# The decode tokens' small steps in both mixers, per head or tile before, for four heads or four tiles together after

## The chip, the cores and the metric

One core of a Trainium2 chip runs the kernel. Its engines are TensorE (PE), VectorE (DVE), ScalarE (ACT), GpSimd (POOL) and the sync engine (SP), which here issues every DMA. The metric is the device time of one execution in microseconds: 1788.39 us before, the median of three runs (1786.42 to 1792.95).

## What is computed

One step of a two-layer network in float32: a prompt of 512 tokens and eight decode tokens, one each of eight sequences with states of their own. Layer 0 has a gated delta rule (GDN) as mixer, layer 1 a state-space scan (SSD); each is followed by a layer norm, a convolutional feed-forward part and another norm. What a decode token needs of the two mixers is one step of their recurrences:

```python
# GDN: per head, state s (DK x DV); q, k l2-normalised, q also scaled by DK ** -0.5
s = exp(g) * s
v_new = beta * (v - k @ s)
o = q @ s + (q . k) * v_new
s = s + outer(k, v_new)

# SSD: per head, state h (P x N); B, C shared by the heads of a group
h = exp(dt * a) * h + dt * outer(x, B)
y = h @ C + D * x
```

The l2 norm of a row t is `t * rsqrt(sum(t * t) + 1e-6)`. In SSD the kernel uses that `y = exp(dt*a) * (h @ C) + dt * x * (B . C) + D * x`, with the old h.

## The kernel before

All 520 tokens go as columns through the weight matmuls, in two halves of 260 (`HT`). A unit is one 128-row tile of outputs: 24 matmuls per half (three for each of eight 128-row tiles of inputs, since weights and inputs are split into a high and a low fp32r part). `prep` loads a weight tile, ScalarE makes `hi` (L223), and VectorE or GpSimd makes `lo` (L224); three tiles are held at a time. The units run in the order of `plan`; between them stand the mixers' own steps.

In GDN the loop over eight heads runs three units (q, k and v columns of the head), copies the decode columns into `kqv`, calls `gdn_decode` for them, and then `gdn_head` and four `gdn_chunk` for the prompt. `gdn_head` multiplies `Xe` on GpSimd (L769), sums it on VectorE to `Ac` (L771), writes that to DRAM, reads it back as `D` and inverts the diagonal blocks by a chain of steps `Xtmp` (L812); after that come triangular solves with small matmuls into `XT`, and the chunks with `st`, `w`, `o`. `gdn_norm` transposes the head's result (`ot`).

`gdn_decode` for one head: GpSimd forms k k and k q (`pr`, 128x8 each) and q q (`qd2`); a matmul with ones sums them over the partitions into PSUM, VectorE copies them to `dk` (L941). k and q are transposed and sent through DRAM (`kr`), to be read back broadcast over the partitions (`kb`, four DMAs of 256 KB a head). GpSimd multiplies these by the old states (L952), VectorE sums each product over its last axis into `ks` (L953). Then eight 128x8 steps on VectorE (L959, L961 to L965, L967 to L969) and one power on GpSimd (L536, exponent -0.5 from the tile `halves`) give `vn` and `ud`. The states themselves are updated later, within the feed-forward part, from `vn`. After the last head `gdn_decode_norm` norms `ud` for heads 0 to 3 and then 4 to 7, and the output projection starts.

In SSD a group g of the four has B, C and four tiles of x, each of two heads. `ssd_group` runs after the group's sixth unit: chunk states, then `ssd_bcast` (B and C of the decode tokens transposed, their product summed on VectorE on eight partitions, L1210 and L1211, and sent through DRAM to `bcd` on all partitions), and then per tile the prompt's decays `sE`, scores `yd` and `yo`, and `ssd_decode`: state times C (GpSimd or VectorE, L1237), summed into `dy` (L1238), three 128x8 steps (L1240 to L1242), and a fourth (L1243) that adds the result into the decode columns of x. The z units that read x come after the next group's six units, in the last group after four others.

The tile framework's scheduler orders the instructions of each engine before the run, by the order of the code, priorities and a timeline of its own, and sets the semaphores. Each engine then works through its list in order.

## Time and profile before

| what | value |
|---|---|
| median of 3 runs | 1788.39 us |
| profiled execution | 1785.41 us |
| its span, first to last instruction | 1783.6 us |
| TensorE busy | 1613.7 us (90%), 12889 matmuls |
| VectorE busy | 1221.2 us (68%), 2133 instructions |
| ScalarE busy | 839.3 us (47%), 1724 |
| GpSimd busy | 968.4 us (54%), 1090 |
| chain that ended last, by engine | PE 30%, DVE 24%, DMA 18%, POOL 14%, ACT 8%, issue 5% |

In forty slices of the span (44.6 us each; a digit is the busy share in tenths) TensorE and VectorE read `8888899888999899999888897989988998889997` and `5967888668876544337699989895569765554356`. GDN lies in the slices 2 to 9, SSD in 20 to 28; the long plateaus of TensorE between and behind them are the feed-forward parts. Matmuls are pipelined, so a busy TensorE is not one at its peak; idle time of an engine that nobody waits for costs nothing.

### The profile page before, as it was taken

The numbers are of one execution on the slowest core, as the hardware profiler recorded it, in microseconds if no ns is written. First come the engines' busy times: TensorE is split into PE (matmuls) and PEld (weight loads), VectorE is DVE, ScalarE is ACT, GpSimd is POOL, SyncE is SP. The second block draws the span as 40 slices with busy tenths as digits, with TensorE's granted clock in tenths as the row PEclk, the third lists the DMA queues.
The fourth block names the chain that finished last, engine by engine and source line by source line (L and its number), as shares of the span: only waits on it lengthen the run. The fifth ranks groups of instructions, "written<-read, shape, count | busy, mean of one in ns | idle before, by whom it ended". The sixth has DMA issues, their size and how long they took to land.

```text
span 1783.6 us, 33737 instructions
## 1 busy us (share of the span) xinstructions
PE 1613.7 (90%) x12889; PEld 1550.4 (87%) x12889; DVE 1221.2 (68%) x2133; ACT 839.3 (47%) x1724; POOL 968.4 (54%) x1090
## 2 busy tenths in 40 slices
PE   8888899888999899999888897989988998889997
...
DVE  5967888668876544337699989895569765554356
...
DMA packets 108978, 250.36 MB, mean 140 GB/s; under 512 B 15344, under 2 KB 31696, under 8 KB 108784
## 3 DMA queue, kind: packets, MB, share of 16 engines
...
## 4 chain that ended last, share of the span: by engine, by line
PE 30%; DVE 24%; DMA 18%; POOL 14%; ACT 8%; issue 5%; SPq 1%; ACTq 0%; DVEq 0%; POOLq 0%
PE psl L246 26%; DVE lo L224 3%; DMA raw<-w_up 3%; DMA Sr<-bd 3%; POOL Sd L990 3%; ACT hi L223 3%; POOL Sr L988 3%; DVE sE L1180 2%; DMA Sr<-kr 2%; DVE y L419 2%; DMA raw<-w_down 2%; POOL Sd L989 2%; POOL fl L279 1%; DVE Xtmp L812 1%; DMA Sd<-sstate 1%
## 5 line engine op out<-in xcount | busy, mean ns | idle before, releaser
L246 PE MATMUL psl<-XH,hi 128*128 128x260 f32 (+1 forms) x2816 | 819.5, 292 | 61.4 <-ACT u L442 18.4
L246 PE MATMUL psl<-XL,hi 128*128 128x260 f32 (+1 forms) x2848 | 823.6, 290 | 8.8 <-DVE lR L308 3.9
L246 PE MATMUL psl<-XH,lo 128*128 128x260 f32 (+1 forms) x2816 | 809.7, 288 | 2.7 <-DVE lo L224 1.6
L246 PEld LDWEIGHTS psl<-XH,hi 128*128 128x128 f32 (+1 forms) x2816 | 538.9, 192 | 78.0 <-ACT u L442 22.0
L224 DVE TENSOR_TENSOR lo<-raw,hi 128x512 fp32r<-128x512 f32 (+2 forms) x439 | 356.9, 850 | 327.7 <-ACT hi L223 323.3
L246 PEld LDWEIGHTS psl<-XL,hi 128*128 128x128 f32 (+1 forms) x2848 | 545.6, 192 | 15.4 <-issue 5.7
L246 PEld LDWEIGHTS psl<-XH,lo 128*128 128x128 f32 (+1 forms) x2816 | 539.2, 192 | 7.6 <-DVE lo L224 3.1
L223 ACT CAST hi<-raw 128x512 fp32r<-128x512 f32 (+2 forms) x499 | 315.2, 671 | 435.0 <-PE psl L246 191.7
L246 PE MATMUL psl<-fh,lo 128*128 128x260 f32 x704 | 201.2, 286 | 1.8 <-DVE lo L224 1.4
L246 PE MATMUL psl<-fh,hi 128*128 128x260 f32 x704 | 200.3, 284 | 0.7 <-ACT hi L223 0.7
L246 PE MATMUL psl<-fl,hi 128*128 128x260 f32 x704 | 198.8, 282 | 0.0
L224 POOL TENSOR_TENSOR lo<-raw,hi 128x1024 fp32r<-128x1024 f32 x60 | 148.6, 2476 | 53.5 <-ACT hi L223 52.1
L246 PEld LDWEIGHTS psl<-fh,lo 128*128 128x128 f32 x704 | 132.5, 188 | 4.0 <-DVE lo L224 3.6
L246 PEld LDWEIGHTS psl<-fh,hi 128*128 128x128 f32 x704 | 132.5, 188 | 1.4 <-ACT hi L223 0.9
L246 PEld LDWEIGHTS psl<-fl,hi 128*128 128x128 f32 x704 | 132.4, 188 | 0.2
L279 POOL TENSOR_TENSOR fl<-f,fh 128x260 fp32r<-128x260 f32 x88 | 80.3, 914 | 66.4 <-ACT fh L278 66.3
L419 DVE SCALAR_TENSOR_TENSOR s<-u,par,s 128x512 f32<-128x512 f32 x88 | 82.6, 939 | 6.8 <-ACT s L416 6.8
L278 ACT CAST fh<-f 128x260 fp32r<-128x260 f32 x88 | 36.0, 409 | 96.5 <-DVE f L481 96.5
L246 PE MATMUL psl<-y,hi 128*128 128x260 f32 x256 | 73.3, 288 | 1.8 <-DVE y L279 0.8
L990 POOL TENSOR_TENSOR Sd<-Sd,Sr 128x512 f32<-128x512 f32 x48 | 70.1, 1460 | 0.5
L365 POOL TENSOR_TENSOR lnsq<-lnsq,sq 128x260 f32<-128x260 f32 x48 | 46.8, 978 | 28.8 <-ACT sq L363 27.3
L471 POOL COPY cout<-u 128x10 f32<-128x10 f32 x44 | 19.2, 436 | 77.7 <-ACT u L442 77.6
...
## 6 DMA issues: line engine op xcount, KB each, us to landing
...
```

The lines of the kernel that those rows point to most:

```text
L223: nc.scalar.copy(out=hi[:, ks, :mw], in_=raw[:, ks, :])
L224: eng.tensor_tensor(out=lo[:, ks, :mw], in0=raw[:, ks, :], in1=hi[:, ks, :mw].bitcast(F32), op=ALU.subtract)
L246: self.nc.tensor.matmul(out=ps[h][:mw], lhsT=w[:, b0 + k, :mw], rhs=x[:, hs], start=(k0 + k == first and i == 0), stop=(k0 + k == last and ...
L278: nc.scalar.copy(out=hi, in_=xf)
L279: (eng or nc.gpsimd).tensor_tensor(out=lo, in0=xf, in1=hi.bitcast(F32), op=ALU.subtract)
L365: nc.gpsimd.tensor_tensor(out=acc, in0=acc, in1=sq, op=ALU.add)
L419: nc.vector.scalar_tensor_tensor(out=y[:, :S], in0=u[:, j:j + S], scalar=self.pcol(wname, i * w + j), in1=y[:, :S], op0=ALU.mult, op1=ALU.add)
L471: nc.gpsimd.tensor_copy(out=cout[:, m, :], in_=u[:, 2 + S - 2:2 + T])
L988: nc.gpsimd.tensor_tensor(out=t, in0=t, in1=_bc(col[:, :, None], D4), op=ALU.mult)
L989: nc.gpsimd.tensor_tensor(out=St, in0=St, in1=_bc(decay[:, :, None], D4), op=ALU.mult)
L990: nc.gpsimd.tensor_tensor(out=St, in0=St, in1=t, op=ALU.add)
L1180: nc.vector.tensor_scalar(out=E[:, c, :], in0=E[:, c, :], scalar1=self.acum[:, c, h:h + 1], scalar2=0.0, op0=ALU.subtract, op1=ALU.min)
```

## The change

GDN: `gdn_decode` keeps what starts the DMAs (transpose, `kr`, `kb`, multiplies and sums, now into the tile `kS` of all heads). The products, the ones matmul, the power and the eight steps move into `gdn_decode_rest`, which is called twice, after `gdn_head` of head 4 for heads 0 to 3 and after that of head 7 for heads 4 to 7, on 128x32 operands. The sums are copied from PSUM by ScalarE instead of VectorE. SSD: `dy` holds the four tiles of a group, and three 128x32 steps and the four final ones run in `ssd_decode_rest` at the group's end. The product B C is formed by GpSimd on all partitions and summed by a matmul with ones; two DMAs a group go. `halves` shrinks to one column per exponent, broadcast by the access pattern. The line numbers behind the change are up to 16 higher.

```diff
...
         nc.sync.dma_start(out=self.par, in_=a["par"])
-        self.halves = p.tile([P, 2, B], F32, name="halves")
-        nc.vector.memset(self.halves[:, 0], -0.5)
-        nc.vector.memset(self.halves[:, 1], 0.5)
+        self.halves = p.tile([P, 2], F32, name="halves")
+        nc.vector.memset(self.halves[:, :1], -0.5)
+        nc.vector.memset(self.halves[:, 1:], 0.5)
         self.mean = p.tile([P, P], F32, name="mean")
...
         n = x.shape[-1]
-        self.nc.gpsimd.tensor_tensor(out=y, in0=x, in1=self.halves[:, which, :n], op=ALU.pow)
+        self.nc.gpsimd.tensor_tensor(out=y, in0=x, in1=_bc(self.halves[:, which:which + 1], [P, n]), op=ALU.pow)
 
...
                     x = self.gdn_head(p, h, st["kq", h], st["v", h], e)
+                    if h in (NA, H - 1):
+                        self.gdn_decode_rest(p, *((0, NA) if h == NA else (NA, H)))
                     for c in range(C):
...
         self.kqv = p.tile([P, H, 3, B], F32, name="kqv")
+        self.kS = p.tile([P, H, 2, B], F32, name="kS")
         self.vn = self.keep.tile([P, H, B], F32, tag="k0", name="vn")
...
         kqv = self.kqv[:, h]
-        k, q, vd = (kqv[:, t, :] for t in range(3))
-        pr = p.tile([P, 2, B], F32, tag="pr", name="pr", bufs=2)
-        nc.gpsimd.tensor_tensor(out=pr[:, 0, :], in0=k, in1=k, op=ALU.mult)
-        nc.gpsimd.tensor_tensor(out=pr[:, 1, :], in0=k, in1=q, op=ALU.mult)
-        nc.gpsimd.tensor_tensor(out=self.qd2[:, h, :], in0=q, in1=q, op=ALU.mult)
         ps = self.sp("dks")
-        nc.tensor.matmul(out=ps[:, P:P + 2 * B].rearrange("p (t b) -> p t b", t=2), lhsT=self.ones, rhs=pr, start=True, stop=True)
         self.transpose(ps[:2 * B, :P], kqv[:, :2, :].rearrange("p t b -> p (t b)"))
...
         nc.scalar.copy(out=rows, in_=ps[:2 * B, :P])
-        dk = p.tile([P, 2, B], F32, tag="dk", name="dk", bufs=2)
-        nc.vector.tensor_copy(out=dk, in_=ps[:, P:P + 2 * B].rearrange("p (t b) -> p t b", t=2))
         kr = self.dram.tile([2, B, P], F32, tag=f"kr{h}", name="kr")
         nc.sync.dma_start(out=kr.rearrange("t b d -> (t b) d"), in_=rows)
-        ks = p.tile([P, 2, B], F32, tag="ks", name="ks", bufs=2)
+        ks = self.kS[:, h]
         for i in range(2):
...
                 nc.vector.tensor_reduce(out=ks[:, t, bs], in_=m, axis=AX.X, op=ALU.add)
-        ps2 = dk
-        sm = p.tile([P, 4, B], F32, tag="sm", name="sm", bufs=2)
-        rk, t, _, t2 = (sm[:, i, :] for i in range(4))
-        vn = self.vn[:, h, :]
-        egh, bh = self.deg[:, h, :], self.dbeta[:, h, :]
-        nc.vector.tensor_scalar(out=t, in0=ps2[:, 0, :], scalar1=1e-6, scalar2=None, op0=ALU.add)
-        self.power(t, rk, 0)
-        nc.vector.tensor_tensor(out=t, in0=rk, in1=egh, op=ALU.mult)
-        nc.vector.tensor_tensor(out=t, in0=t, in1=ks[:, 0, :], op=ALU.mult)
-        nc.vector.tensor_tensor(out=vn, in0=vd, in1=t, op=ALU.subtract)
-        nc.vector.tensor_tensor(out=vn, in0=vn, in1=bh, op=ALU.mult)
-        nc.vector.tensor_tensor(out=vn, in0=vn, in1=rk, op=ALU.mult)
-        u = self.ud[:, h, :]
-        nc.vector.tensor_tensor(out=t, in0=ks[:, 1, :], in1=egh, op=ALU.mult)
-        nc.vector.tensor_tensor(out=t2, in0=vn, in1=ps2[:, 1, :], op=ALU.mult)
-        nc.vector.tensor_tensor(out=u, in0=t, in1=t2, op=ALU.add)
         for i in range(2):
...
 
+    def gdn_decode_rest(self, p, h0, h1):
+
+        nc = self.nc
+        n = h1 - h0
+        hs = slice(h0, h1)
+        k, q, vd = (self.kqv[:, hs, t, :] for t in range(3))
+        ks = self.kS[:, hs]
+        pr = p.tile([P, 2, n, B], F32, tag="pr", name="pr", bufs=1)
+        nc.gpsimd.tensor_tensor(out=pr[:, 0], in0=k, in1=k, op=ALU.mult)
+        nc.gpsimd.tensor_tensor(out=pr[:, 1], in0=k, in1=q, op=ALU.mult)
+        nc.gpsimd.tensor_tensor(out=self.qd2[:, hs, :], in0=q, in1=q, op=ALU.mult)
+        ps = self.sp("drms")[:, :2 * n * B]
+        nc.tensor.matmul(out=ps, lhsT=self.ones, rhs=pr.rearrange("p t h b -> p (t h b)"), start=True, stop=True)
+        dk = p.tile([P, 2, n, B], F32, tag="dk", name="dk", bufs=1)
+        nc.scalar.copy(out=dk, in_=ps.rearrange("p (t h b) -> p t h b", t=2, b=B))
+        sm = p.tile([P, 3, n, B], F32, tag="sm", name="sm", bufs=1)
+        rk, t, t2 = (sm[:, i] for i in range(3))
+        vn, u = self.vn[:, hs, :], self.ud[:, hs, :]
+        eg, bh = self.deg[:, hs, :], self.dbeta[:, hs, :]
+        tt = lambda o, x, y, op: nc.vector.tensor_tensor(out=o, in0=x, in1=y, op=op)
+        nc.vector.tensor_scalar(out=t, in0=dk[:, 0], scalar1=1e-6, scalar2=None, op0=ALU.add)
+        flat = lambda x: x.rearrange("p h b -> p (h b)")
+        self.power(flat(t), flat(rk), 0)
+        tt(t, ks[:, :, 0, :], eg, ALU.mult)
+        tt(t, t, rk, ALU.mult)
+        tt(vn, vd, t, ALU.subtract)
+        tt(vn, vn, bh, ALU.mult)
+        tt(vn, vn, rk, ALU.mult)
+        tt(t, ks[:, :, 1, :], eg, ALU.mult)
+        tt(t2, vn, dk[:, 1], ALU.mult)
+        tt(u, t, t2, ALU.add)
+
     def gdn_state(self, p, after, h, i, kr):
...
         bcs = self.ssd_bcast(p, g, Bt, Ct)
+        yd4 = p.tile([P, 4, B], F32, tag="dy", name="dy", bufs=2)
         for q in range(4):
...
                 nc.sync.dma_start(out=ea[64 * s:64 * s + 64], in_=self.ade[h0 + s].rearrange("c t -> (c t)").partition_broadcast(64))
-            self.ssd_decode(p, g, q, x, bcs)
+            self.ssd_decode(p, g, q, x, bcs, yd4)
             d = self.pcol("sd", 4 * g + q)
...
             nc.gpsimd.tensor_tensor(out=x[:, P:S], in0=x[:, P:S], in1=ea[:, P:], op=ALU.add)
+        self.ssd_decode_rest(p, g, bcs[1], yd4)
 
...
         nc.scalar.copy(out=bc, in_=ps[:B, :2 * P].rearrange("p (t n) -> p t n", t=2))
-        t = p.tile([B, P + 1], F32, tag="bct", name="bct", bufs=2)
-        nc.vector.tensor_tensor(out=t[:, :P], in0=bc[:, 0, :], in1=bc[:, 1, :], op=ALU.mult)
-        nc.vector.tensor_reduce(out=t[:, P:], in_=t[:, :P], axis=AX.X, op=ALU.add)
+        t = p.tile([P, 2, B], F32, tag="bcd", name="bcd", bufs=2)
+        nc.gpsimd.tensor_tensor(out=t[:, 0], in0=Bt[:, S:], in1=Ct[:, S:], op=ALU.mult)
+        nc.tensor.matmul(out=ps[:, 2 * P:2 * P + B], lhsT=self.ones, rhs=t[:, 0], start=True, stop=True)
+        nc.scalar.copy(out=t[:, 1], in_=ps[:, 2 * P:2 * P + B])
         bd = self.dram.tile([2, B, P], F32, tag=f"bd{g}", name="bd")
...
             nc.sync.dma_start(out=bd[i], in_=bc[:, i, :])
-        cd = self.dram.tile([B, 1], F32, tag=f"cd{g}", name="cd")
-        nc.sync.dma_start(out=cd, in_=t[:, P:])
         c = p.tile([P, B, P], F32, tag="cbc", name="cbc", bufs=2)
         nc.sync.dma_start(out=c, in_=bd[1].rearrange("b n -> (b n)").partition_broadcast(P))
-        d = p.tile([P, B], F32, tag="bcd", name="bcd", bufs=2)
-        nc.sync.dma_start(out=d, in_=cd.rearrange("b o -> (b o)").partition_broadcast(P))
-        return c, d, bd
+        return c, t[:, 1], bd
 
-    def ssd_decode(self, p, g, q, x, bcs):
+    def ssd_decode(self, p, g, q, x, bcs, y):
 
...
         nc.vector.tensor_tensor(out=xd, in0=x[:, S:], in1=self.ddt[:, :, 0, i], op=ALU.mult)
-        y = p.tile([P, B], F32, tag="dy", name="dy", bufs=2)
-        t = p.tile([P, B], F32, tag="dyt", name="dyt", bufs=2)
         for j in range(2):
...
             (nc.vector if (i + j) % 3 == 2 else nc.gpsimd).tensor_tensor(out=Sd, in0=Sd, in1=c[:, bs], op=ALU.mult)
-            nc.vector.tensor_reduce(out=y[:, bs], in_=Sd, axis=AX.X, op=ALU.add)
+            nc.vector.tensor_reduce(out=y[:, q, bs], in_=Sd, axis=AX.X, op=ALU.add)
             self.later.append((self.ssd_state, i, j, bd))
-        nc.vector.tensor_tensor(out=y, in0=y, in1=self.ddt[:, :, 1, i], op=ALU.mult)
-        nc.vector.tensor_tensor(out=t, in0=xd, in1=cb, op=ALU.mult)
+
+    def ssd_decode_rest(self, p, g, cb, y):
+
+        nc = self.nc
+        gs = slice(4 * g, 4 * g + 4)
+        t = p.tile([P, 4, B], F32, tag="dyt", name="dyt", bufs=2)
+        nc.vector.tensor_tensor(out=y, in0=y, in1=self.ddt[:, :, 1, gs].rearrange("p b i -> p i b"), op=ALU.mult)
+        nc.vector.tensor_tensor(out=t, in0=self.xdd[:, gs], in1=_bc(cb[:, None, :], [P, 4, B]), op=ALU.mult)
         nc.vector.tensor_tensor(out=y, in0=y, in1=t, op=ALU.add)
-        nc.vector.scalar_tensor_tensor(out=x[:, S:], in0=x[:, S:], scalar=self.pcol("sd", i), in1=y, op0=ALU.mult, op1=ALU.add)
+        for q in range(4):
+            x = self.Y(4 * g + q)[:, S:]
+            nc.vector.scalar_tensor_tensor(out=x, in0=x, scalar=self.pcol("sd", 4 * g + q), in1=y[:, q], op0=ALU.mult, op1=ALU.add)
```

The scheduler places the instructions of both mixers anew; those of the two feed-forward parts stand as before. Three places, each before and then now.

VectorE, head 0 of GDN: from the decode chain to the reduction `Ac`, the start of the head's inversion.

```order
L963 TENSOR_TENSOR vn<-kqv,sm 128x8
L964 TENSOR_TENSOR vn<-vn,dbeta 128x8
L965 TENSOR_TENSOR vn<-vn,sm 128x8
L968 TENSOR_TENSOR sm<-vn,dk 128x8
L953 TENSOR_REDUCE ks<-kb 128x4
L967 TENSOR_TENSOR sm<-ks,deg 128x8
L914 TENSOR_SCALAR nt<-sq 128x4
L969 TENSOR_TENSOR ud<-sm 128x8
L771 TENSOR_REDUCE Ac<-Xe 128x64
```

```order
L768 TENSOR_TENSOR gbc<-gbc,kqk 128x256
L419 SCALAR_TENSOR_TENSOR kq<-u,par,kq 128x512
L948 TENSOR_REDUCE kS<-kb 128x4
L774 TENSOR_REDUCE Ac<-Xe 128x64
L775 TENSOR_TENSOR Ac<-Ac,Xi 128x64
```

The chain of head 0 has left the rows ahead of `Ac`; the sum into `kS` (L948, then L953) stays.

GpSimd, end of GDN: the powers (`halves`) and the last head's four multiplies into `kb`; L580 multiplies a head's result by z.

```order
L536 TENSOR_TENSOR nf<-nt,halves 128x4
L536 TENSOR_TENSOR sm<-sm,halves 128x8
L952 TENSOR_TENSOR kb<-kb,Sd 128x512 x3
L580 TENSOR_TENSOR R<-R,z 128x260
L580 TENSOR_TENSOR R<-R,z 128x252
L952 TENSOR_TENSOR kb<-kb,Sd 128x512
L582 COPY R<-z 128x8
```

```order
L536 TENSOR_TENSOR nf<-nt,halves 128x4
L921 TENSOR_TENSOR uo<-uo,nf 128x512
L947 TENSOR_TENSOR kb<-kb,Sd 128x512 x4
L580 TENSOR_TENSOR R<-R,z 128x260
L580 TENSOR_TENSOR R<-R,z 128x252
L582 COPY R<-z 128x8
L536 TENSOR_TENSOR nf<-nt,halves 128x4
L536 TENSOR_TENSOR sm<-sm,halves 128x32
L947 TENSOR_TENSOR kb<-kb,Sd 128x512 x4
```

One power of 32 columns now stands ahead of head 7's multiplies, where one of eight columns stood. On TensorE the last head's `ot` transposes stand behind 1,674 unit matmuls of the program, 1,620 before; the 96 of the output projection's first part end at 1,680 in both.

VectorE, group 1 of SSD: the steps of `dy` (`xdt`, `ea`, `sE` and `Sn` belong to the prompt).

```order
L1238 TENSOR_REDUCE dy<-Sd 128x4
L1154 TENSOR_TENSOR xdt<-xtk,dt 128x4x128
L1240 TENSOR_TENSOR dy<-dy,ddt 128x8
L1154 TENSOR_TENSOR xdt<-xtk,dt 128x4x128
L1242 TENSOR_TENSOR dy<-dy,dyt 128x8
L1238 TENSOR_REDUCE dy<-Sd 128x4
L1197 SCALAR_TENSOR_TENSOR y<-y,par,yd 128x512
L1243 SCALAR_TENSOR_TENSOR y<-y,par,dy 128x8
L1241 TENSOR_TENSOR dyt<-xdd,bcd 128x8
L1198 TENSOR_TENSOR ea<-ea,yo 128x384
L1238 TENSOR_REDUCE dy<-Sd 128x4
```

```order
L1246 TENSOR_REDUCE dy<-Sd 128x4
L224 TENSOR_TENSOR lo<-raw,hi 128x1024
L1254 TENSOR_TENSOR dy<-dy,ddt 128x32
L1256 TENSOR_TENSOR dy<-dy,dyt 128x32
L1259 SCALAR_TENSOR_TENSOR y<-y,par,dy 128x8 x4
L1176 TENSOR_TENSOR Sn<-Sn,sst 128x512
```

Per tile there were four steps between the prompt's; now three for the group and the four final ones (L1243, now L1259) stand together behind its last sum.

## Rows read from the trace of the kernel before

**Rows 1.** Stretches: PE, PEld, DVE, ACT, POOL busy (count); clock; DMA share; GB/s

```profile
700.00:750.00 50.00, 50.00 (x419) 50.00 (x418) 16.26 (x29) 13.05 (x27) 12.78 (x15) 1.00 0.30 88
60.00:400.00 340.00, 301.58 (x2549) 286.02 (x2547) 258.90 (x601) 174.72 (x501) 221.13 (x252) 0.94 0.33 100
880.00:1215.00 335.00, 290.44 (x2179) 267.42 (x2178) 295.77 (x498) 184.90 (x271) 208.00 (x167) 0.95 0.43 136
```

**Rows 2.** PE's waits, GDN then SSD: engine line, releaser: us, times, longest

```profile
PE z L847 <- DVE XT L840: 4.8, 1, 4.8
...
PE kqk L762 <- DVE vn L964: 0.3, 1, 0.3
...
PE xtk L512 <- DVE xdt L1154: 8.7, 4, 2.9
...
PE cb L1139 <- DVE rowa L1122: 0.9, 1, 0.9
```

**Rows 3.** Single lines, ns minimum/median/maximum of one

```profile
L536 POOL TENSOR_TENSOR rk<-ss,halves x8: 1002/1011/1469, 65.4 to 303.5; 128x4 f32<-128x4 f32 x8
L536 POOL TENSOR_TENSOR sm<-sm,halves x8: 1635/1637/2107, 72.4 to 376.9; 128x8 f32<-128x8 f32 x8
...
L964 DVE TENSOR_TENSOR vn<-vn,dbeta x8: 154/166/1039, 85.1 to 389.9; 128x8 f32<-128x8 f32 x8
```

**Rows 4.** Timeline of DVE: start us, us, instruction

```profile
81.23 2.02 DVE L962 TENSOR_TENSOR sm<-sm,ks 128x8 f32<-128x8 f32 x1
...
90.47 1.06 DVE L771 TENSOR_REDUCE Ac<-Xe 128x64 f32<-128x512 f32 x1
...
365.29 0.68 DVE L224 TENSOR_TENSOR lo<-raw,hi 128x512 fp32r<-128x512 f32 x1
```

**Rows 5.** Timeline of POOL in the same stretches and at the end of GDN

```profile
80.39 2.84 POOL L224 TENSOR_TENSOR lo<-raw,hi 128x1024 fp32r<-128x1024 f32 x1
...
85.18 1.29 POOL L769 TENSOR_TENSOR Xe<-M,cn 128x512 f32<-128x512 f32 x1
...
364.05 1.64 POOL L536 TENSOR_TENSOR sm<-sm,halves 128x8 f32<-128x8 f32 x1 [1.43 <-DVE sm L959]
...
376.88 1.64 POOL L536 TENSOR_TENSOR sm<-sm,halves 128x8 f32<-128x8 f32 x1 [1.07 <-DVE sm L959]
380.80 3.73 POOL L952 TENSOR_TENSOR kb<-kb,Sd 128x512 f32<-128x512 f32 x3 [2.29 <-DMA kb<-kr]
```

**Rows 6.** DVE and POOL busy on the tile sm, by stretch

```profile
60.00:400.00 340.00, 38.71 (x64) 14.06 (x8) 0.94 0.33 100
```

**Rows 7.** Groups of DVE: count, busy us, mean ns, idle before

```profile
L1240 DVE TENSOR_TENSOR dy<-dy,ddt 128x8 f32<-128x8 f32 x16 | 9.7, 607 | 0.1
...
L964 DVE TENSOR_TENSOR vn<-vn,dbeta 128x8 f32<-128x8 f32 x8 | 2.6, 322 | 0.0
...
L941 DVE COPY dk<-dks 128x16 f32<-128x16 f32 x8 | 1.3, 164 | 0.8 <-ACT vr L939 0.8
...
L999 DVE TENSOR_TENSOR dnt<-ud 128x32 f32<-128x32 f32 x2 | 0.4, 192 | 0.1
```

**Rows 8.** DVE busy on the tile dyt, by stretch

```profile
880.00:1215.00 335.00, 16.55 (x32) 0.95 0.43 136
```

**Rows 9.** PE, PEld, DVE, ACT busy on the tile bct

```profile
880.00:1215.00 335.00, 1.69 (x8) 0.69 (x8) 3.25 (x8) 1.41 (x4) 0.95 0.43 136
```

**Rows 10.** Chain of waits that ended last, single pieces: start us, us, what

```profile
81.31 1.95 DVE sm L962
...
90.40 0.15 DVE ud L969
...
389.93 0.09 DVE vn L964
...
918.14 0.19 DVE bct L1210
...
1198.59 0.08 DVE dyt L1241
```

## The prediction, made before the changed kernel ran

> **What bounds the kernel now.** I read the engines by stage first, then what TensorE waits for, then the two engines that it waits for, in order of time. In a stretch of feed-forward work (700 to 750 us) TensorE is busy throughout: 419 matmuls in 50 us, 0.119 us each [rows 1]. In the GDN mixer (60 to 400 us) it is busy for 301.58 of 340 us and in the SSD mixer (880 to 1215 us) for 290.44 of 335, both at a mean granted clock below 1; VectorE (DVE) is busy for 258.90 us (76%) and 295.77 us (88%) there [rows 1]. So only these two stages have slack to give. What TensorE waits for there is VectorE above all: in GDN twelve rows of the waits, from 4.8 us (on `XT`) down to 0.3 us, 25.6 us in sum; in SSD eleven rows, from 8.7 us (on `xdt`) down to 0.9 us, 39.3 us [rows 2].
>
> What VectorE does in those stages shows in its timeline beside GpSimd's (POOL). Around 81 us the 128x8 steps of head 0's decode chain take 1 to 2 us each, though the same form needs 0.154 us at the least [rows 3]. They end when a GpSimd instruction ends: L962 (81.23, 2.02 us) at 83.25, GpSimd's weight split at 80.39 + 2.84 = 83.23 [rows 4, 5]. A tiny step with two SBUF operands waits out a whole GpSimd instruction, and a chain of them moves at GpSimd's pace. The change makes one such chain of four.
>
> **What goes, GDN.** Per head ten VectorE steps: L941 (moved to ScalarE, once per four heads), L959, L961 to L965, L967 to L969. Eight lines touch `sm`: 38.71 us for 64 instructions; L964 adds 2.6 and L941 1.3: 42.6 us for 80 instructions [rows 6, 7]. Undisturbed, at 0.16 us, they would be 12.8; the other 29.8 us are waits, 0.37 us a step. Two blocks of nine 128x32 steps come instead. The only such tensor_tensor of the trace, L999, takes 0.19 us [rows 7]; with the same wait each is 0.56, eighteen are 10.1 us (3.4 if none waits). Net -32.5 us of VectorE.
>
> **What goes, SSD.** Per tile L1240 to L1242: 16.55 us in 32 for the two that touch `dyt`, 9.7 us in 16 for L1240; per group the two steps on `bct`, 3.25 us in 8 [rows 7 to 9]. 29.5 us for 56. Twelve 128x32 steps at 0.56 come: 6.7. Net -22.8 us. The final step per tile stays, sixteen of them, now at the end of the group; nobody reads the decode columns before the z units, at least four units later.
>
> **What of it lies on the path.** In the chain of work that ended last, the GDN lines that go are 32 pieces, the first of 1.95 us at 81.31, the last of 0.09 us at 389.93, 23.7 us in sum, 56% of their 42.6; the SSD lines 31 pieces, from 918.14 to 1198.59, 10.3 us, 35% of their 29.5 [rows 10]. The same shares of the net figures are 18.2 and 8.0, 26.2 us. Not all comes out at the end, since something else is late next. Head 0 shows how much: from 81.31 to 90.55 seven small steps, L962 to L969, are 7.8 us of that chain [rows 10], and behind them stands L771, the reduction to `Ac`, from which the diagonal blocks are inverted. It reads `Xe`, which GpSimd finishes at 85.18 + 1.29 = 86.47 [rows 5]. Without the chain L771 starts at 86.5 at the earliest instead of 90.47 [rows 4]: 4.0 of 7.8 us, about half. I take half throughout: -13 us. Bounds: the whole 26 us, or a quarter (6.5) if GpSimd, whose instructions do not get fewer there, is late next everywhere.
>
> **GpSimd.** The power L536 takes 1.011 us for four columns and 1.637 for eight (medians, [rows 3]): 0.157 us a column on 0.385, so about 5.4 us for 32. This is an estimate from two widths; the lower bound is one 1.64 us power as before, the upper 4 x 1.64 = 6.6. Two instead of eight, 10.8 us for about 13.1, but in lumps. Queued behind the first are a weight split and head 3's multiplies, in mid-pipeline, where the split's consumer has further weights in stock; no charge. Behind the second stand head 7's four multiplies, near the end of GDN. There the power of eight columns ran at 376.88, and GpSimd later idled 2.29 us for the rows `kb` [rows 5]. Of the 3.8 us that are added this hides 2.3; I charge 1.5 us, and 0.5 us for the block of six steps in a row that now stands ahead of `M` in head 5. Whether the long power blocks VectorE: at 364.05 to 365.69 one ran, and a VectorE split with two SBUF operands, 0.68 us from 365.29, ended at 365.97, 0.28 us after the power [rows 4, 5]; it did not wait it out. So I charge nothing.
>
> The Trainium skill (SBUF — State Buffer, "Who interferes with whom") says that the shared pair is held for a whole instruction and that a two-input VectorE instruction then fully blocks; by it two powers could cost VectorE up to 10.8 us where eight cost up to 13.1 before, which would leave the sum as it is, and the overlap at 365.29 speaks against it.
>
> **The rest.** The ones matmuls (eight fewer in GDN, two and four more) and ScalarE's copies (six more) are 0.2 to 0.4 us each and lie beside dense work: nothing, or 2 us if every one were exposed. A new wait is TensorE's on GpSimd's product in front of the SSD matmul: unit matmuls queue behind it, but it stands some twenty rows after the transposes; nothing, bounded by one weight split ahead of it, four times 2.4 us. On the sync engine's queue eight small DMAs go with their waits for `bct` and for each other; loads of `sE`, `Sd` and weights queue behind. No gain is booked for it.
>
> **Sum.** 1785.4 us (the profiled execution; span 1783.6 and 1.8 around it) - 13 + 2 = 1774.4. The median of the runs lies 3.0 us higher, at 1788.4, so the same sum from there is 1777.4. I forecast 1776.
>
> **Rivals.** *The whole chain comes out*: 26 us less 2, and some clock back, since in both stages the mean granted clock is 0.94 and 0.95 [rows 1]; 1785.4 - 24 = about 1761. For it: 65 us of TensorE's waits name VectorE. Against: head 0's half.
>
> *Only SSD gives*: in GDN, VectorE has a quarter of its time free and latency rules, so that one long chain late is no better than four early; then half of SSD's 8.0 remains, less 2: 1783, within the bound. The stage's 76% speaks for it, the 7.8 us at head 0 against. The Trainium skill (Perfetto Trace Analysis, "Optimizing Scalar/DVE Operations") says that grouping into larger operations helps a saturated engine, and that on one that is not saturated but causes bubbles elsewhere smaller pieces may finish sooner. By that rule the same 1783 would come out.
>
> *Slower, by GDN's end*: the order puts the last head's `ot` transposes behind 1,674 unit matmuls instead of 1,620. TensorE runs through its units sooner and then stands before head 7. Price: 54 x 0.119 = 6.4 us of cover gone, the power's full 3.8, and nine waiting steps (5.0 us) where the last eight took some 1.4; 13.8 us. If the earlier gain of GDN is only waited off there, and SSD gives 2, the time is about 1797. It decides from the point at which GDN's end loses 9 us more than all else gains. For it: the chain's last piece at 389.93 [rows 10] shows that the decode steps were on the path at that end. Against: GpSimd's 2.29 us of slack there [rows 5], and heads that start earlier.
>
> **How the numbers follow.** Forecast (half comes out) 0.47, its own range 1768 to 1783; whole chain 0.16; SSD only, or a quarter, 0.25; slower by GDN's end 0.12. A measurement of this kernel tells about 0.5%, 8.9 us, from no change, so the bounds are 1779.4 and 1797.3 us. Faster: 0.16 and some 0.44 of the 0.47, 0.60. Within: the rest of the forecast, the third case and part of the last, 0.30. Slower: 0.10. Range 1760 to 1791: from the whole chain to halfway into the last case, about one in ten outside on either side.
>
> **What would show it right or wrong.** Right: VectorE's busy time down by some 30 us in GDN and 20 in SSD, with fewer tiny steps that end with a GpSimd instruction; `Ac` of head 0 some 4 us sooner; less waiting of TensorE on `XT`, `X`, `xdt`, `Sn`. A power near 5.4 us. Wrong: VectorE relieved but both stages as long, with GpSimd or DMA named in the waits; the steps after the removed ones taking over their waits; TensorE idle longer before the output projection; or the 128x32 steps each far above 0.56 us.

## The result: 0.75% slower

The changed kernel took 1800.46 us, in its median and in the profiled execution (span 1798.7), against 1788.39. The ratio over the seven runs of each is 1.0075, interval 1.0056 to 1.0093. The forecast was 1776 in a range up to 1791; the sign was wrong and the time lies 9.5 us above the range.

First two stretches of [rows 1], GDN and SSD, now of the changed kernel, with 400 to 500 us (the output projection and the norm behind GDN) beside them; then that stretch before. Columns as in [rows 1]: TensorE, its weight loads, VectorE, ScalarE and GpSimd busy, then the granted clock.

```profile
60.00:400.00 340.00, 300.07 (x2511) 284.53 (x2511) 248.06 (x533) 170.50 (x496) 214.49 (x227) 0.93 0.32 97
400.00:500.00 100.00, 85.73 (x648) 81.72 (x647) 77.11 (x134) 53.46 (x115) 39.61 (x51) 0.95 0.49 152
880.00:1215.00 335.00, 289.50 (x2148) 266.21 (x2148) 292.60 (x461) 189.74 (x286) 198.70 (x169) 0.93 0.43 136
```

```profile
400.00:500.00 100.00, 89.67 (x684) 86.69 (x685) 81.98 (x145) 57.24 (x121) 38.90 (x55) 0.97 0.51 158
```

Read the counts of TensorE first. In 60 to 400 us it got 2511 matmuls done instead of 2549, in 400 to 500 us 648 instead of 684, 74 fewer. Twelve of these are small matmuls that the change itself took out (tiles `dks` and `drms`: 28 before, 16 after). What is behind are unit matmuls, tile `psl`. Counted over 60 to 500 us at once (in two stretches a matmul that runs across 400 us counts twice), before, then after (here the columns are PE, PEld, DVE, ACT, clock):

```profile
60.00:500.00 440.00, 281.93 (x1989) 259.75 (x1988) 6.58 (x17) 27.92 (x75) 0.95 0.37 113
...
60.00:500.00 440.00, 274.22 (x1925) 250.61 (x1925) 6.50 (x16) 26.73 (x72) 0.93 0.36 110
```

64 unit matmuls behind are 7.6 us at 0.119 us each [rows 1], and five more were behind at 60 us already. That is most of the lag in the feed-forward part behind it: there, at 700 us, the same instructions start 8.8 us later (median over matched instructions). Behind SSD, at 1265 us, the lag is 8.5. After that it grows by another 6 in this one execution, with the same order of instructions, around two short episodes at half clock (1497 and 1637 us). So in these two profiles GDN and what follows it at once lost the time. SSD lost none beside it, though a gain was forecast there; the runs of the SSD half alone, below, put its loss at 0.28%.

Then VectorE. It is busy for 248.06 and 292.60 us where it was for 258.90 and 295.77 [rows 1]: 10.8 and 3.2 us less, where 32.5 and 22.8 were forecast. The removed work did go. Below, the tile `sm` in GDN (VectorE, GpSimd) and `dyt` in SSD, for [rows 6, 8]:

```profile
60.00:400.00 340.00, 6.94 (x16) 10.83 (x2) 0.93 0.32 97
...
880.00:1215.00 335.00, 3.42 (x7) 0.93 0.43 136
```

38.71 became 6.94 and 16.55 became 3.42. What took its place shows in two tiles whose instructions the change leaves as they are: `Xtmp` in GDN and `sE` in SSD (columns PE, PEld, DVE, ACT, POOL where the engine touches the tile). Before, then after:

```profile
60.00:400.00 340.00, 45.22 (x128) 0.94 0.33 100
...
880.00:1215.00 335.00, 32.70 (x256) 26.83 (x256) 69.18 (x144) 19.91 (x32) 24.18 (x16) 0.95 0.43 136
```

```profile
60.00:400.00 340.00, 50.24 (x128) 0.93 0.32 97
...
880.00:1215.00 335.00, 32.85 (x242) 26.40 (x243) 91.91 (x144) 19.86 (x32) 23.50 (x16) 0.93 0.43 136
```

The same 128 steps on `Xtmp` take 5.0 us more, and the same 144 VectorE instructions on `sE` 22.7 us more, as much as SSD's relief was to be (in `x_none` below, whose SSD is the old one, they take 72.42). One pair of rows shows how. Two multiplies of one form on VectorE, and the GpSimd instruction beside the second:

```profile
956.28 0.68 DVE L1196 TENSOR_TENSOR sE<-sE,CB 128x512 f32<-128x512 f32 x1
...
958.74 2.24 DVE L1196 TENSOR_TENSOR sE<-sE,CB 128x512 f32<-128x512 f32 x1
...
958.04 2.39 POOL L224 TENSOR_TENSOR lo<-raw,hi 128x1024 fp32r<-128x1024 f32 x1 [2.35 <-ACT hi L223]
```

The first takes 0.68 us. The second stands beside GpSimd's weight split, which ends at 958.04 + 2.39 = 960.43, and ends 0.55 us behind it. So I read the wait as one that goes with GpSimd's instruction and not with the step that meets it: if the `dy` steps are gone, the next VectorE step meets the split. The sum over all steps bears this out. I added up, for VectorE instructions that end at most 0.6 us behind the end of a GpSimd one, what they take beyond a short run of their form: in GDN (60 to 430 us) 78.5 us before and 74.9 after, in SSD (885 to 1225) 100.0 and 96.5. (With 0.3 us as the bound it is 63 and 53 in GDN, 72 and 69 in SSD.) GpSimd's work stayed, but for 6.6 and 9.3 us of busy time, and so did most of the waits. Which step meets them changes with the order: `s_bcast` below takes only the two `bct` steps (3.25 us [rows 9]) off VectorE, and `sE` takes 81.23 us in it, but 69.59 in `s_bc2`. So the 22.7 us of `sE` are not those of the removed steps one by one; the sum is the reading to go by.

Where TensorE now waits in SSD (engine, line, what released it: us, times, longest), for [rows 2]:

```profile
PE yo L1202 <- DVE Sn L1178: 11.8, 3, 8.7
...
PE xtk L512 <- DVE xdt L1165: 7.4, 3, 3.3
PE bct L1224 <- ACT bc L1221: 2.9, 1, 2.9
```

8.0 us on `Sn` (L1167, now L1178) became 11.8, 8.7 on `xdt` became 7.4, and 2.9 us are new: the ones matmul waits, not for GpSimd's product as the prediction had it, but for ScalarE's copy out of the same PSUM tile.

### The profile page after: what moved, and what is told of

It is laid out like the page before. It is cut to its first block, busy times and chain, and to the rows that moved or that the text cites. A ratio compares the mean times of both kernels' runs of the same rounds, so it can differ in the third digit from the quotient of the medians.

```text
span 1798.7 us, 33601 instructions
## 1 busy us (share of the span) xinstructions
PE 1620.9 (90%) x12885; PEld 1556.6 (87%) x12885; DVE 1211.8 (67%) x2027; ACT 838.0 (47%) x1730; POOL 956.2 (53%) x1070
## 4 chain that ended last, share of the span: by engine, by line
PE 31%; DVE 26%; DMA 18%; POOL 13%; ACT 5%; issue 5%; SPq 1%; ACTq 0%; DVEq 0%; POOLq 0%
PE psl L246 26%; DVE lo L224 4%; DVE sE L1192 3%; DMA raw<-w_up 3%; POOL Sd L1001 3%; POOL Sr L999 3%; DMA Sr<-bd 2%; ACT hi L223 2%; DVE y L419 2%; POOL Sd L1000 2%; DMA Sd<-sstate 2%; DMA raw<-w_down 2%; POOL fl L279 2%; DVE Xtmp L815 1%; DMA Sr<-kr 1%
## 5 line engine op out<-in xcount | busy, mean ns | idle before, releaser
L224 POOL TENSOR_TENSOR lo<-raw,hi 128x1024 fp32r<-128x1024 f32 x60 | 147.3, 2455 | 64.3 <-ACT hi L223 62.8
L419 DVE SCALAR_TENSOR_TENSOR s<-u,par,s 128x512 f32<-128x512 f32 x88 | 89.4, 1015 | 8.5 <-ACT s L416 8.1
L1192 DVE TENSOR_SCALAR sE<-sE,acum 128x128 f32<-128x128 f32 x128 | 72.2, 625 | 3.1 <-DMA sE<-ad 3.0
```

Of the source, the lines that this page charges most:

```text
L224: eng.tensor_tensor(out=lo[:, ks, :mw], in0=raw[:, ks, :], in1=hi[:, ks, :mw].bitcast(F32), op=ALU.subtract)
L419: nc.vector.scalar_tensor_tensor(out=y[:, :S], in0=u[:, j:j + S], scalar=self.pcol(wname, i * w + j), in1=y[:, :S], op0=ALU.mult, op1=ALU.add)
L1192: nc.vector.tensor_scalar(out=E[:, c, :], in0=E[:, c, :], scalar1=self.acum[:, c, h:h + 1], scalar2=0.0, op0=ALU.subtract, op1=ALU.min)
```

## What moved in GDN: the order on VectorE

The change did more than take steps away. The scheduler ordered VectorE's list anew, and with the decode steps gone it put other steps ahead of the path. Around 240 us head 4 is in its inversion chain (`Xtmp` of 16 to 128 columns) and head 5 begins: `M` in two halves, then `Ac`, from which its own inversion starts. Timeline of VectorE before (start, us, instruction):

```profile
244.51 0.41 DVE L764 TENSOR_TENSOR M<-gbc,kqk 128x256 f32<-128x256 f32 x1
...
248.43 0.17 DVE L812 TENSOR_TENSOR Xtmp<-X,D 128x16 f32<-128x16 f32 x1
...
248.72 0.41 DVE L764 TENSOR_TENSOR M<-gbc,kqk 128x256 f32<-128x256 f32 x1
...
251.80 1.04 DVE L771 TENSOR_REDUCE Ac<-Xe 128x64 f32<-128x512 f32 x1
...
257.81 0.29 DVE L812 TENSOR_TENSOR Xtmp<-X,D 128x128 f32<-128x128 f32 x1
```

and after:

```profile
233.93 0.16 DVE L815 TENSOR_TENSOR Xtmp<-X,D 128x16 f32<-128x16 f32 x1
...
248.14 0.41 DVE L767 TENSOR_TENSOR M<-gbc,kqk 128x256 f32<-128x256 f32 x1
...
254.36 0.28 DVE L815 TENSOR_TENSOR Xtmp<-X,D 128x128 f32<-128x128 f32 x1
...
255.74 0.41 DVE L767 TENSOR_TENSOR M<-gbc,kqk 128x256 f32<-128x256 f32 x1
...
259.98 1.06 DVE L774 TENSOR_REDUCE Ac<-Xe 128x64 f32<-128x512 f32 x1
```

Before, the first `M` stood ahead of the chain, the second behind one of its eight multiplies, `Ac` behind four. Now the first `M` stands behind five, the second behind all eight, and `Ac` starts at 259.98 instead of 251.80. (A later place in the list is not lateness by itself: head 4's two `M` went from behind none and two multiplies of head 3's chain to behind five and seven, and its `Ac` came sooner, at 217.8 instead of 221.0.) In short form, from the lists of VectorE (`c1` to `c8`: multiplies of head 4's chain, each with its sum; `q`, `k`: convolutions of head 7's columns; `v`: other convolutions):

```
before:  q  M  c1  M  c2 c3 c4  Ac  c5  k  c6 c7 c8
after:   c1  v  c2  q  c3 c4 c5  M  c6  k  c7 c8  M  Ac
```

Head 5 is late from there, and heads 6 and 7 with it. One row tells it: the `xt` transposes of the last heads on TensorE, first and last start. Before:

```profile
L512 PE MATMUL xt<-cn,X x12: 270/273/328, 295.1 to 347.6; 128*128 128x128 f32 x12
```

After:

```profile
L512 PE MATMUL xt<-cn,X x12: 272/273/474, 303.8 to 358.6; 128*128 128x128 f32 x12
```

They start 8.7 us and end 11.0 us later. (The first decode steps, in the meantime, gave what they were to give: `Ac` of head 0 starts at 86.38 instead of 90.47, and the first `xt` at 118.5 instead of 121.4.)

Between 250 us and the last `ot` there is a second part. This stretch is 142.5 us long before and 153.0 after; TensorE sits idle for 14.7 and 14.0 us of it, no more than before, but 27.3 instead of 13.7 us of it are at half clock. The stretches of after around one such place (columns as above):

```profile
325.00:330.00 5.00, 4.90 (x43) 4.49 (x42) 4.64 (x14) 2.00 (x7) 2.02 (x3) 1.00 0.06 14
330.00:335.00 5.00, 3.26 (x28) 2.76 (x28) 1.57 (x2) 1.92 (x4) 2.73 (x3) 1.00 0.87 263
335.00:340.00 5.00, 3.55 (x17) 3.55 (x17) 2.74 (x5) 0.00 (x0) 2.73 (x2) 0.64 0.80 214
340.00:345.00 5.00, 5.00 (x52) 4.49 (x52) 2.37 (x7) 0.55 (x3) 2.51 (x3) 0.50 0.13 47
345.00:350.00 5.00, 4.89 (x31) 3.96 (x27) 2.41 (x12) 1.81 (x6) 0.00 (x0) 0.50 0.02 5
```

and what TensorE did there (in brackets: idle before it, and what ended that):

```profile
332.22 1.11 PE L877 MATMUL u<-Vc,XT 128*128 128x128 f32 x8
336.45 1.76 PE L838 MATMUL xz<-Z,XT 128*128 128x64 f32 x7 [3.12 <-DVE Z L835]
```

It had run through the unit matmuls that were ready (the last one before 330 us, the next at 354), then stood 3.12 us for `Z` of a late head, and the clock fell to 0.50, which is the lower of its two levels (1.2 of 2.4 GHz), while it worked off the head's small matmuls. Before, the longest stretch without a unit matmul there was about 10 us. By the code it can't just take further units: a z unit's result is multiplied by the head's normed result on GpSimd (L580), so the z units wait for the heads. From 60 to 430 us GpSimd sat idle 12.3 us for that ScalarE result (L926) after, 4.8 before.

## The experiments

All ratios are to the kernel before, with 95% intervals, on the chip of that comparison; about 0.2% can be told.

**Which half.** `e1_gdn` has the GDN part of the change alone, `e2_ssd` the SSD part alone.

> Only the GDN half of the change; the SSD code and its instruction order are those of before. Theory A (the new order of GDN costs cover): in the changed kernel the last three heads' solves stand behind 1382, 1488 and 1512 unit matmuls instead of 1335, 1391 and 1488, and the trace shows the first feed-forward part some 9 us late; this kernel has the same order, so it should be 8 to 12 us slower than before, about 1797 to 1800 us. Theory B (the SSD half costs it, since the prompt's steps take over the waits behind GpSimd): within 3 us of before. The prediction's own sum for this half was -9 us plus 2.

> Only the SSD half; GDN's code and order are those of before. Theory A: no loss here, within 4 us of before (the SSD stage is 335 us long in the changed kernel's trace to within 2 us of before). Theory B: the whole loss of some 12 us, about 1800. The prediction's sum for this half was -4 us.

GDN alone: 1.0065 (1.0042 to 1.0088). SSD alone: 1.0028 (1.0012 to 1.0045). Both halves lose, GDN most; SSD's 5.0 us (1795.84 against 1790.83) lie between what the two theories gave. In SSD alone the waits of TensorE read:

```profile
PE yo L1191 <- DVE Sn L1167: 13.1, 3, 8.7
PE yo L1191 <- DVE ea L1199: 7.1, 2, 4.8
```

On `Sn` 13.1 us stand for 8.0 before, on `ea` 7.1 for 4.9 (the same view). The steps on `sE` are again the longer ones: L1181 is busy for 71.6 us, as L1180 for 52.8 before.

**Where the blocks stand, and their size.** `g_late2` puts both blocks behind the loop's last unit; `g_one` makes eight blocks of one head each, each behind its `gdn_head`.

```diff
-                    if h in (NA, H - 1):
-                        self.gdn_decode_rest(p, *((0, NA) if h == NA else (NA, H)))
+                    self.gdn_decode_rest(p, h, h + 1)          # g_one
...
+                for h in (0, NA):                               # g_late2, behind the loop
+                    self.gdn_decode_rest(p, h, h + NA)
```

> e1_gdn with both blocks of the batched decode steps moved behind the last head and the last unit of the loop. The last three solves then stand behind 1309, 1438 and 1536 unit matmuls and the last head's transposes behind 1587 (1674 in e1_gdn, 1620 before). Theory A (order, cover at the end): 8 us or more faster than e1_gdn, at or under the time of before, 1780 to 1790. Theory C (the blocks' own length, two powers of 5.4 us and eighteen VectorE steps, costs where it stands on the path): both blocks now stand in a row in front of the output projection, so not faster than e1_gdn, 1798 to 1808.

> e1_gdn with one block per head (128x8 operands, power of eight columns) behind each head's gdn_head: nothing is batched, the new tile and ScalarE's copy stay. Its order is close to before's (last transposes behind 1620 unit matmuls, last solves behind 1302, 1390, 1487). Theory A: time of before, 1783 to 1793. Theory C (the batch itself is what costs): the same, so it tells A from C only beside g_late2. If copy and tile matter by themselves: above 1795.

`g_late2`: 1.0112 (1.0083 to 1.0141), slower still: to take the blocks off the last heads' way doesn't bring the time back. Theory A is missed by some 20 us (1809.56), and C's "not faster" is met. `g_one`: 1.0043 (1.0024 to 1.0063), with steps of the old size. From 250 us to the last `ot` it needs 146.3 us, 142.5 before, 157.7 in `e1_gdn`. Why it is slower than before at all stays open.

**No chain at all, and TensorE's order.** `x_none` leaves the small steps of GDN's decode tokens out (`vn`, `ud` and `qd2` are filled with 0.01; the states' sums stay). `p_e1` is GDN alone with the last z units held behind given heads in TensorE's list.

```diff
+        for t in (self.vn, self.ud, self.qd2):                  # x_none
+            nc.vector.memset(t, 0.01)
...
+                behind = {3: 5, 4: 6, 5: 6, 6: 7, 7: 7}         # p_e1: z unit -> last xt of head
+                            es.enter_context(tc.issue_after(self.xts[behind[j]]))
```

> e1_gdn with the decode tokens' small steps of GDN left out altogether (vn, ud and qd2 are constants; products, ones matmul, power and all 128x8 or 128x32 steps are gone, the states' multiplies and sums stay). It bounds what the removal can bring. The prediction's account (the removed waits come out): 13 to 24 us below before, 1765 to 1778. Theory D (a wait belongs to the GpSimd instruction, and VectorE's next step takes it over): VectorE's steps that end with a GpSimd instruction still carry 65 us or more of waiting in GDN (78 in before), and the time is within 6 us of before.

> e1_gdn with TensorE's order put back by hand: z units 3, 4 and 5, 6 and 7 are queued behind the transposes into xt of heads 5, 6 and 7, so that these stand behind 1344, 1392 and 1488 unit matmuls as in before (1335, 1391, 1488), not 1382, 1488, 1512. The work is that of e1_gdn. Theory A (the new order took the cover from the last heads): 8 us or more faster than e1_gdn, within 4 us of before. If besides the prediction's saving is real, it now shows: 1778 or less. Theory C (length and place of the blocks cost it): no change against e1_gdn, 1798 to 1806.

`x_none`: 1.0081 (1.0056 to 1.0105). A kernel without the steps, without their power and without any block is as slow as the changed one, 15 us above the one before (1805.93), where the prediction's account had it 13 to 24 below and theory D within 6. So a loss of this size needs neither the power nor the nine steps in a row; what these cost beside it can't be seen here. (The waits behind GpSimd, added up as above, are 64.3 us in it, about D's 65.) Its `xt`:

```profile
L512 PE MATMUL xt<-cn,X x12: 272/273/328, 294.9 to 363.4; 128*128 128x128 f32 x12
```

`p_e1`: 1.0093 (1.0068 to 1.0118). With the z units in about the old place (1344, 1392 and 1488 unit matmuls of the program stand ahead of the `xt` of heads 5, 6 and 7; 1335, 1391 and 1488 before) the time is not back: `xt` runs from 304.1 to 355.4, in `e1_gdn` from 306.1 to 359.5, before from 295.1 to 347.6. TensorE's list alone is not the cause (theory A had this run 8 us faster than `e1_gdn`; it is 1806.88 us). That led to VectorE's.

**Order on VectorE.** The scheduler takes an order between two instructions of one engine without a wait or a semaphore. `c_b` is the kernel before with the two `M` of head 5 held behind the fifth and the last multiply of head 4's chain, as in the new order. `r3_e1` is GDN alone with three chains held behind the next head's `M` and one convolution of head 7 behind head 5's `M`, which is near the old order; `r4_e1` adds the z units' places; `x_r4` is `x_none` with the same pins as `r4_e1`.

```diff
+            b = {(5, 0): (4, 6), (5, 1): (4, 0)}.get((h, half))           # c_b
+            if b:
+                self.tc.add_manual_dep(self.steps["M", h], self.steps[("chain",) + b].name,
...
+            for (a, i), g in {(4, 14): 5, (5, 14): 6, (3, 12): 4}.items():  # r3: chain behind M
+                if (half, h) == (1, g):
+                    self.tc.add_manual_dep(self.steps["chain", a, i], self.steps["M", h].name,
...
+                behind = {1: ('kqk', 6), 4: ('xt', 6), 5: ('xt', 6), 6: ('xt', 7), 7: ('xt', 7)}  # r4
```

> The reverse: the kernel before, every step as it was, with one pin: head 5's two steps M are held on VectorE behind the fifth and the last multiply of head 4's inversion chain, as they stand in the changed kernel. The rest of the order follows by itself (last solves behind 1340, 1472, 1530 unit matmuls). Theory E: 6 to 14 us slower than before, 1797 to 1805, with longer stretches at half clock at the end of GDN. If the order has no weight: within 3 us of before.

> The work of e1_gdn (GDN half of the change). In the changed kernel's trace heads 0 to 4 come up to 3 us sooner, but heads 5, 6 and 7 reach their transposes into xt 9, 15 and 11 us later, since on VectorE head 4's inversion chain (Xtmp) and two convolutions of head 7 now stand ahead of head 5's M and Ac. Here VectorE's order is put back by hand: the chains of heads 3, 4 and 5 behind M of heads 4, 5 and 6, and one convolution of head 7 behind M of head 5. Theory E (it is VectorE's order that delays the last heads): 6 us or more faster than e1_gdn, 1788 to 1796. Theory D alone (waits behind GpSimd pass on, order without weight): as e1_gdn, 1798 to 1806.

> r3_e1 with TensorE's order put back as well (z unit 1 behind head 6's kqk, z units 4 and 5 and 6 and 7 behind the transposes into xt of heads 6 and 7). Theory E: as before the change or a few us better, 1782 to 1792; the prediction's full saving of this half would be 1780. If order has no weight: 1798 to 1806.

> x_none (the decode tokens' small steps of GDN left out; vn, ud and qd2 are constants) with the pins of r4_e1. It prices the removed work at an order like that of before. Theory E with D: 1780 to 1790, that is 0 to 10 us below before, and 15 us or more below x_none. The prediction's account would have it at 1765 to 1778.

`c_b`: 1.0086 (1.0067 to 1.0104). All work of the kernel before, two steps moved in VectorE's list, and 15.4 us (0.0086 x 1791) are lost, as much as by the whole change. TensorE's list moved along by itself: 1340, 1472 and 1530 unit matmuls stand ahead of the `xt` of heads 5, 6 and 7. So `c_b` prices the order of both engines. Its VectorE and its `xt`:

```profile
249.61 0.41 DVE L766 TENSOR_TENSOR M<-gbc,kqk 128x256 f32<-128x256 f32 x1
...
254.50 0.29 DVE L819 TENSOR_TENSOR Xtmp<-X,D 128x128 f32<-128x128 f32 x1
...
255.25 0.41 DVE L766 TENSOR_TENSOR M<-gbc,kqk 128x256 f32<-128x256 f32 x1
...
262.69 1.00 DVE L778 TENSOR_REDUCE Ac<-Xe 128x64 f32<-128x512 f32 x1
```

```profile
L512 PE MATMUL xt<-cn,X x12: 272/273/327, 299.9 to 361.6; 128*128 128x128 f32 x12
```

The second `M` at 255.25 and `Ac` at 262.69 stand as in the changed kernel, and the last heads are as late (361.6).

`r3_e1`: 1.0040 (1.0025 to 1.0056); `r4_e1`: 1.0000 (0.9983 to 1.0016). In `r4_e1` the loss of the GDN half is gone with its order: the work is that of `e1_gdn` (1.0042 to 1.0088), and the intervals lie apart. `r3_e1` is a miss of theory E (1798.23 us, where 1788 to 1796 were expected), and its interval meets that of `e1_gdn`: that VectorE's order alone brings time back is not shown. Nor did TensorE's alone (`p_e1`); the two together do. `r4_e1`:

```profile
240.72 0.41 DVE L776 TENSOR_TENSOR M<-gbc,kqk 128x256 f32<-128x256 f32 x1
...
242.87 0.42 DVE L776 TENSOR_TENSOR M<-gbc,kqk 128x256 f32<-128x256 f32 x1 [0.34 <-PE kqk L773]
...
249.32 1.03 DVE L788 TENSOR_REDUCE Ac<-Xe 128x64 f32<-128x512 f32 x1
...
254.67 0.29 DVE L829 TENSOR_TENSOR Xtmp<-X,D 128x128 f32<-128x128 f32 x1
```

```profile
L512 PE MATMUL xt<-cn,X x12: 271/273/421, 293.1 to 341.4; 128*128 128x128 f32 x12
```

Both `M` stand ahead of the chain, `Ac` behind two of its multiplies (four before), and the last heads start earlier than before. What `r3_e1` still lacked was the z units' places: 0.4% of the time. The kernel before was not run with all of these orders, so that they suit the old work better than its own order is not ruled out; with the pins of `u_spread`, three z units fewer, it stayed as it was (`b_spread` below, 1.0009).

`x_r4`: 0.9947 (0.9932 to 0.9963). `x_none` and `x_r4` do the same work; their medians are 1805.93 and 1782.41 us, 23.5 us apart by order alone (the kernel before stood at 1790.95 and 1791.20 beside them). And in an order like the old one the removal of the steps is worth 0.0053 x 1791 = 9.5 us, 6.6 to 12.2 by the interval.

```profile
L512 PE MATMUL xt<-cn,X x12: 270/272/328, 288.8 to 338.9; 128*128 128x128 f32 x12
```

From `x_r4` to `r4_e1`, 1782.41 to 1790.88, is what the two blocks cost with these pins: 8.5 us, nearly all that the removal brings. The lists are not quite the same even so (1297 and 1346 unit matmuls stand ahead of head 5's `xt`). Next: is it the power?

**The power, and the whole change.** `r5_e1` is `r4_e1` with ScalarE and VectorE (`rsqrt`) instead of GpSimd's two powers; `r4_full` is the whole change with the pins of `r4_e1`.

```diff
-        nc.vector.tensor_scalar(out=t, in0=dk[:, 0], scalar1=1e-6, scalar2=None, op0=ALU.add)
-        self.power(flat(t), flat(rk), 0)
+        self.rsqrt(rk, dk[:, 0], 1e-6)
```

> r4_e1 with the 32-column power taken off GpSimd: VectorE adds 1e-6 and takes the reciprocal, ScalarE the square root. r4_e1 stood at 1.000 of before and x_r4, without any of the steps, at 0.995, so the two blocks cost some 8.5 us at that order. If the two powers of 5.4 us, in front of the last heads' multiplies into kb, are most of it: 3 to 9 us below r4_e1, 1782 to 1788. If the eighteen VectorE steps and their place are: as r4_e1, 1788 to 1794.

> The whole change with the pins of r4_e1. The halves add up so far (1.0065 and 1.0028 against 1.0075 for the whole); if they still do, the whole loss of GDN goes and that of SSD stays: 1.001 to 1.004 of before, 1792 to 1798. If the order of GDN were not the cause: 1.006 or more.

`r5_e1`: 0.9995 (0.9980 to 1.0009), not to be told from `r4_e1`: taking the power off GpSimd brought nothing. It isn't quite cleared by this, since the list behind the pins is another one here too: head 7's `Ac` stands behind all eight multiplies of head 6's chain, behind three in `r4_e1`. `r4_full`: 1.0048 (1.0032 to 1.0065), where `r4_e1` and `e2_ssd` sum up to 1.0028; the intervals meet. But so do those of `r4_full` and of the changed kernel (1.0056 to 1.0093): that the old order helps the whole change is shown for its GDN half, and not by this run.

**SSD apart.** `s_bcast` is the kernel before with the new `ssd_bcast` (ones matmul) only, `s_batch` with the steps for four tiles only, `s_bc2` is `s_bcast` with the product formed first and the ones matmul ahead of ScalarE's copy.

```diff
+        t = p.tile([P, 2, B], F32, tag="bcd", name="bcd", bufs=2)      # s_bc2: ahead of the copy
+        nc.gpsimd.tensor_tensor(out=t[:, 0], in0=Bt[:, S:], in1=Ct[:, S:], op=ALU.mult)
...
+        nc.tensor.matmul(out=ps[:, 2 * P:2 * P + B], lhsT=self.ones, rhs=t[:, 0], start=True, stop=True)
```

> Before with only the new sum of B C (GpSimd's product, the matmul with ones, ScalarE's copy; VectorE's two steps and two small DMAs a group are gone). If TensorE's wait in front of that matmul (3.0 us in one group of e2_ssd's trace) is what costs: 3 to 5 us slower than before. If the batch is: within 2 us of before.

> Before with only the batched steps on dy per group (12 instead of 48, the four final ones at the group's end). If moving the waits onto the steps sE delays the scores that TensorE waits for: 3 to 5 us slower than before. If the matmul is what costs: within 2 us of before. The prediction gave this part some 3 us of gain.

> s_bcast with the matmul with ones put ahead of ScalarE's copy of the transposes, so that it no longer stands behind that copy in the same PSUM tile. s_bcast was at 1.0022 of before with a wait of TensorE of 3.2 us there. If that wait is the cost: 0.999 to 1.001 of before. If the reordered stage behind it is: 1.001 to 1.004, and the waits on Sn and sE are found again.

`s_bcast`: 1.0022 (1.0004 to 1.0040); `s_batch`: 1.0003 (0.9985 to 1.0020); `s_bc2`: 1.0011 (0.9992 to 1.0031). The four tiles together change nothing; the SSD half's loss points to the ones matmul. Its wait for ScalarE (3.2 us in `s_bcast`) is gone from the rows of `s_bc2`, but the interval of `s_bc2` can't tell it from either: whether that wait is the loss stays open.

**Is it the unit matmuls' spread?** A theory on the half clock was that the time hangs on how evenly the unit matmuls lie between the last heads. `u_spread` (GDN alone, VectorE as in `r3_e1`, z units so placed that 1346, 1435 and 1488 unit matmuls stand ahead of those `xt`), `q_spread` (the same aim with `rsqrt`: 1339, 1414 and 1488) and `b_spread` (the kernel before with the pins of `u_spread`: 1305, 1371 and 1488) test it.

```diff
-                behind = {1: ('kqk', 6), 4: ('xt', 6), 5: ('xt', 6), 6: ('xt', 7), 7: ('xt', 7)}
+                behind = {1: ('kqk', 6), 6: ('xt', 7)}                 # u_spread
```

> r4_e1 with fewer pins on TensorE (z unit 1 behind head 6's kqk, z units 6 behind the transposes of head 7; not 4, 5 and 7), so that the unit matmuls are spread more evenly between the heads' solves. In its trace r4_e1 is 9 us ahead of before at 300 us and level at 450, and has a stretch of 17 us without unit matmuls (305 to 322) with 13.7 us at half clock in it. If that stretch gives the gain back: 3 to 8 us below before, 1783 to 1788. If the blocks' own steps do: as r4_e1, 1788 to 1794.

> The GDN half with the reciprocal and square root of r5_e1 in place of the 32-column power, VectorE's pins, and z unit 6 alone behind head 7's transposes; the longest stretch of solve steps without unit matmuls in the order is the shortest of all. Bare stretches as the cause: 1782 to 1788. Otherwise as r5_e1, 1787 to 1793.

> The control for the pins: the kernel before with exactly the pins of u_spread, no step changed. If pins alone bring something: 2 us or more below before. Otherwise within 3 us of it (1788 to 1794), and what u_spread gains over it belongs to the batch.

1.0063 (1.0041 to 1.0084), 1.0089 (1.0066 to 1.0111) and 1.0009 (0.9990 to 1.0028). The theory falls; `u_spread` and `q_spread` are slower than either of their two forecasts. And with the same pins on both, the batched work is 8.8 us slower than the old (1799.40 and 1790.59): the pins alone don't make the GDN half harmless, and since the lists between them differ, this is no clean price of the blocks either. In `u_spread` the mixer itself is back, but the stretch behind it is not:

```profile
250.00:400.00 150.00, 133.87 (x1163) 125.42 (x1161) 98.53 (x247) 70.28 (x214) 92.85 (x88) 0.95 0.34 103
400.00:500.00 100.00, 84.08 (x598) 79.34 (x597) 74.91 (x133) 51.54 (x108) 35.92 (x49) 0.90 0.46 145
```

From 250 us to the last `ot` it needs 141.1 us (142.5 before), and 250 to 400 us have a clock of 0.95 as before; but 400 to 500 us have 0.90 for 0.97, and 598 matmuls for 684. What is saved in the heads is paid at the joint to the output projection. Which order there is the good one can't be read from these runs.

## Why the prediction was wrong, step by step

**The sizes held.** The power of 32 columns, estimated at 5.4 us from two widths:

```profile
L536 POOL TENSOR_TENSOR sm<-sm,halves x2: 5414/5414/5414, 262.7 to 376.7; 128x32 f32<-128x32 f32 x2
```

5.414 us twice. That it doesn't block VectorE's weight split held too, in all seven traces that have such a split beside a power of 32 columns; below the power, the multiplies behind it, and a VectorE split with two SBUF operands that ran its 0.63 us inside the power's time (376.72 to 382.13):

```profile
376.72 5.41 POOL L536 TENSOR_TENSOR sm<-sm,halves 128x32 f32<-128x32 f32 x1 [1.98 <-DVE sm L972]
382.10 2.49 POOL L947 TENSOR_TENSOR kb<-kb,Sd 128x512 f32<-128x512 f32 x2
...
381.22 0.63 DVE L224 TENSOR_TENSOR lo<-raw,hi 128x512 fp32r<-128x512 f32 x1
```

The Trainium skill (SBUF — State Buffer, "Who interferes with whom") would have had it blocked. This row, as the one at 365.29 [rows 4], speaks against that for the power, while the multiply at 958.74 above did wait out GpSimd's weight split. The last head's multiplies start 1.3 us later than before (382.10, 380.80 [rows 5]), against 1.5 charged. The 128x32 steps take 0.41 us on average in GDN (7.4 us for 18), where 0.56 were forecast. `Ac` of head 0 came at 86.38 (86.5 at the earliest).

**The first step that failed: VectorE's relief.** The waits were booked as the removed steps' own: 0.37 us a step, in GDN 29.8 of the 42.6 us. They went with GpSimd's instructions, and most passed to other steps: VectorE's busy time fell by 10.8 and 3.2 us instead of 32.5 and 22.8. Even `x_r4`, where nothing takes the steps' place, has VectorE (third column) busy for only 14.4 us less than before, about the 12.8 that the prediction gave the steps without their waits. (GpSimd's instructions did get fewer in GDN, 252 [rows 1] to 227, where the prediction says that they do not; their busy time fell by 6.6 us.) `x_r4`:

```profile
60.00:400.00 340.00, 300.07 (x2583) 285.60 (x2582) 244.48 (x525) 177.17 (x509) 204.90 (x224) 0.95 0.34 103
```

The last part of the prediction named this as a sign that would prove it wrong. For SSD it takes the whole term: half of 8.0 us was to come out, and the SSD half lost 0.28%, its batch alone measured 1.0003 (0.9985 to 1.0020).

**The second, and the one that turned the sign: the sum was made on the old order.** The prediction looked at the order for single places (head 0, GDN's end), not for what stands ahead of `M` and `Ac` of the late heads. That costs 15.4 us on the old kernel (`c_b`, TensorE's list included), 23.5 between `x_none` and `x_r4`, and all of the GDN half's 0.65% between `e1_gdn` and `r4_e1`.

**The third: the blocks' price.** For an order near the old one the sum has two parts that the runs took apart. The bare removal was to bring half of 23.7 us, 11.9, and `x_r4` measured 9.5. That is near, but partly luck, since the waits that it counted on stayed. The blocks were to take 2.8 us of this (10.1 x 0.56 / 2) and 2 us of charges; they took 8.5 in `r4_e1`. The nine steps at 0.41 (7.4 us for both blocks) could make that up, but no run shows that they do. What was left was 0.0 us (`r4_e1`, 1.0000), where 9.1 less 2 were forecast for GDN.

**The rivals.** "Slower, by GDN's end" had the sign, the place and nearly the time (1797), but another mechanism: longer power, nine waiting steps, fewer units as cover. Without the power the time is the same (`r5_e1`), and the loss comes without any block (`x_none`). The cover did shrink; putting it back alone helped nothing (`p_e1`), with VectorE's order put back as well it brought 0.4% (`r3_e1` to `r4_e1`). "Only SSD gives" is what GDN looks like in a pinned order (`r4_e1`, 1.0000), only that SSD doesn't give either.

**What stays open**: `g_one`'s 1.0043; why `r4_e1`, 6.2 us ahead at the last `xt` (341.4 against 347.6), is level with before at the last `ot` (392.2 and 392.5); whether the kernel before would gain by the whole order of `r4_e1`; why `r4_full` still loses 0.48%; the joint between GDN and the output projection; which part of the ones matmul costs in SSD; the 6 us that the one profile of the changed kernel lost after 1265 us. No kernel that does the whole work was faster than the one before by more than the noise.
